# A mixture-of-experts stage: the overflow branch late, pair units first, the fixed experts' gather in halves

## The chip, the core and the metric

The kernel runs on one core of a Trainium2 chip. The metric is the device time of one execution in microseconds (us). The engines are TensorE (PE), VectorE (DVE), ScalarE (ACT), GpSimd (POOL) and SyncE (SP). Each takes its own instructions in the order of its queue and waits for the others through semaphores.

## What is computed

A backbone of two layers over 512 tokens of width 1024, all in float32. Each layer has a token mixer (attention and spatial gating in layer 0, a short convolution in layer 1) and then a mixture of experts. Only the mixture is touched by the change:

```python
g_idx = argmax(h @ w_rg + b_rg)                       # one of 4 groups
top_v, top_i = top_k(e_logits[group g_idx], 2)        # 2 of its 8 experts
gate = softmax(g_logits)[g_idx] * softmax(top_v)
for each expert e, over the tokens sent to it:
    hid = silu(x @ w_gate[e]) * (x @ w_up[e])         # 1024 -> 512
    y   = hid @ w_down[e]                             # 512 -> 1024
out[token] += gate * y
lat = lat + g2 * out
```

There are 32 experts per layer with 6 MB of weights each (w_gate and w_up as two tiles of 1 MB each, w_down as two), so 384 tiles of 1 MB for the two layers. 1024 assignments are spread over the 32 experts by the router, so how many tokens an expert has is known on the chip only.

## The kernel before

`channel` runs once per layer: `finish_mixer` ends the mixer's output projection, makes the normalised tokens `hv`, `lv` (high and low part), routes them (`Route.block`, `rank`) and starts the loads of the two fixed experts; `experts` then streams the experts' weights.

**Units.** The experts are sorted by their count on the chip. Line 30's PLAN is a row of letters, one per unit: F is one of two fixed experts (64 slots, weights loaded ahead), T one expert with 128 slots, S one with 64, C a pair of experts with 32 slots each. Units are worked off in the order of the letters. `gather` (L1132 ff., products on L1147) brings the tokens of a group of units together with a one-hot product: 64 matmul instructions for 256 slots, then `inform` for weights and token numbers. `up` (L1220, for a T unit L1226) is the first product, of 4 tiles per expert in two halves of two; `mid` transposes and applies SiLU (L1235 to L1245, for T to L1257); `down` (L1274) is the second product, of 2 tiles per expert, and its result is scattered into `acc` in DRAM by an indirect DMA on POOL (L966). In the loop of `experts` unit i does `up(i)`, `down(i-1)`, a few steps of the next gather, `mid(i)`.

**The ring.** `loaded` (L1188 to L1207) issues each weight tile on SP into a ring of 11 slots: two in a `big` buffer (a pair of tiles), five in `raw` buffers, four in two more `big` buffers. A slot is free when PE has read the tile that was in it; the buffers of one pool go round in the order of allocation. A stage has 180 such tiles, besides the 12 tiles of the two fixed experts that `finish_mixer` loads (L741): five into raw buffers, four into two big ones, three into wp buffers. A DMA also waits until the one eight places before it on SP has landed, since SP's DMAs take eight semaphores in turn.

**The overflow branch.** Where an expert has more tokens than its slots, `overflow` (L969 ff.) works off the rest in loops. Each engine loads the count `ovi` into a register (L973) and jumps over the loops if it is zero (L974). With these inputs it is zero in both layers. Before the change it stands ahead of unit 3, and its weight tile `w` is one of the raw buffers.

**The fixed experts' gather.** `gather_first` (L1095 ff.) makes the one-hot product for both fixed experts in two halves of 512 columns (L1105), copies them to `rows` (ACT L1110, DVE L1108), transposes eight blocks (L1120) and modulates them: the second four on ACT (L1090), the first four by two DVE passes over all of them (L1125, L1127). Between them stands the rest of the sort (`Route.sort`, L894 to L962): the slot tables X and info, and the overflow count.

Of the kernel before, what the change touches and what calls it, by code (L numbers as in the profile page):

```python
# [9 lines left out]
F32 = mybir.dt.float32  # L10
# [4 lines left out]
OP = mybir.AluOpType  # L15
# [10 lines left out]
FIX = 2  # L26
RING = 11


PLAN = "FF SCSC TSC SSC TSC SSC TC SCSS".replace(" ", "")  # L30
SLOTS, WIDTH, UNITS = [], [], []
_next = {"F": 0, "T": 2, "S": 5, "C": 16}
for _c in PLAN:
# [59 lines left out]
def backbone_kernel(ctx: ExitStack, tc: tile.TileContext, a, out):  # L93
# [723 lines left out]
    class Route:  # L817
# [77 lines left out]
        def sort(self, ep):  # L895
            tl, rt, xdg, cnt = self.tl, self.rt, self.xdg, self.cnt

            def bc(x, n):
                return x[:, :, None].to_broadcast([128, 4, n])

            kc = tl([128, 1], "kc")
            V.scalar_tensor_tensor(kc[0:96], cnt[0:96, 32:33], 32.0, C("kbcol")[0:96], op0=OP.mult, op1=OP.add)
            kr = tl([128, 32], "kr")
            V.scalar_tensor_tensor(kr[0:96], cnt[0:96, 0:32], 32.0, C("kbrow")[0:96], op0=OP.mult, op1=OP.add)
            V.tensor_scalar(kr[0:96], kr[0:96], kc[0:96], None, op0=OP.is_gt)
            pos = tl([128, 1], "pos")
            V.tensor_reduce(pos[0:96], kr[0:96], AX.X, OP.add)
            perm = tl([128, 3, 32], "perm", bufs=1)
            V.memset(perm, 0.0)
            for j in range(3):  # L910
                q = slice(32 * j, 32 * j + 32)
                V.tensor_scalar(perm[q, j, :], C("rank")[q], pos[q], None, op0=OP.is_equal)
            yield
            po = bankB()
            T.matmul(po[0:1, 0:32], lhsT=C("iop")[0:32], rhs=perm[0:32, 0, :], start=True, stop=True)
            T.matmul(po[0:1, 32:64], lhsT=cnt[0:32, 32:33], rhs=perm[0:32, 0, :], start=True, stop=True)
            V.tensor_copy(rt["ordi"], po[0:1, 0:32])
            ov = tl([1, 32], "ov")
            V.tensor_tensor(ov, po[0:1, 32:64], C("cap")[0:1], OP.subtract)
            yield  # L920
            V.tensor_copy(xdg[:, :, 32:64], bc(C("tok"), 32))
            e2 = tl([128, 4], "e2")
            A.activation(e2, self.dm, AF.Exp)
            gw = tl([128, 4], "gw")
            V.reciprocal(gw, self.gs)
            den = tl([128, 4], "den")
            V.tensor_scalar(den, e2, 1.0, None, op0=OP.add)
            V.reciprocal(den, den)
            w1 = tl([128, 4], "w1")
            V.tensor_tensor(w1, gw, den, OP.mult)  # L930
            w2 = tl([128, 4], "w2")
            V.tensor_tensor(w2, w1, e2, OP.mult)
            V.tensor_tensor(self.A1, self.A1, bc(w1, 32), OP.mult)
            V.tensor_tensor(self.A2, self.A2, bc(w2, 32), OP.mult)
            V.tensor_tensor(xdg[:, :, 64:96], self.A1, self.A2, OP.add)
            px = bankB()
            for b in range(NB):
                T.transpose(px[0:96, b * 128:(b + 1) * 128], xdg[:, b, :], ident)
            xT = ep.tile([128, 512], F32, tag="gy", name="xTr", bufs=2)
            A.activation(xT[0:96], px[0:96], AF.Copy)  # L940
            pq = bankB()
            pqv = pq[:, :384].rearrange("p (b c) -> p b c", b=4)
            for b in range(NB):
                T.matmul(pqv[:, b, :], lhsT=xT[0:96, b * 128:(b + 1) * 128],
                         rhs=perm[0:96].rearrange("p a b -> p (a b)"), start=True, stop=True)
            V.tensor_copy(rt["X"], pqv[:, :, 0:32])

            def infos(dst, n, ix, wt):
                V.tensor_copy(dst[:, :, :, 0], ix)
                A.activation(dst[:, :, :, 1], wt, AF.Copy)  # L950
                V.tensor_tensor(dst[:, :, :, 2], wt, dst[:, :, :, 1].bitcast(F32), OP.subtract)
                V.tensor_copy(dst[:, :, :, 3], one[:, :, None].to_broadcast([128, 4, n]))

            infos(rt["info"], 32, pqv[:, :, 32:64], pqv[:, :, 64:96])
            infos(rt["infoF"], FIX, xdg[:, :, 32:32 + FIX], xdg[:, :, 64:64 + FIX])
            ovc = ep.tile([1, 32, 8], F32, tag="gy", name="ovc", bufs=2)
            V.tensor_tensor(ovc, ov[:, :, None].to_broadcast([1, 32, 8]), C("c64")[0:1, None, :].to_broadcast([1, 32, 8]),
                            OP.is_gt)
            nx = tl([1, 33], "nx")
            V.tensor_reduce(nx[:, 0:32], ovc, AX.X, OP.add)  # L960
            V.tensor_reduce(nx[:, 32:33], nx[:, 0:32], AX.X, OP.add)
            V.tensor_copy(rt["ovi"], nx)  # L962

    def scatter(acc, y, ix):

# [3 lines left out]
    def overflow(l, ep, hv, lv, rt, acc):  # L969

        X, info, ordi, ovi = rt["X"], rt["info"], rt["ordi"], rt["ovi"]
        why = "a count or an index made on the chip"
        any_over = nc.values_load(ovi[0:1, 32:33], min_val=0, max_val=256, skip_runtime_bounds_check_because=why)  # L973
        with pool("o%d" % l, 1) as op, tc.If(any_over > 0):  # L974
# [6 lines left out]
            ixi = op.tile([64, 1], I32)  # L981
            xw = wp.tile([128, 2048], F32, name="wp")
            xt = xw[:, 0:512].rearrange("p (k s) -> p k s", k=8)
            w = rawp.tile([128, 2048], F32, name="raw")
            sl = ep.tile([64, 512], F32, tag="gy", name="slo", bufs=2)
            ht = ep.tile([128, 4, 64], F32, tag="ht", name="hto")
            y = ep.tile([64, 1024], F32, tag="gy", name="yo", bufs=2)
# [52 lines left out]
    def experts(l, ep, ec, hv, lv, early, rt, acc, following):  # L1040
# [46 lines left out]
            def modulated(o, src, k, on_act):  # L1087
                g, h = gcol[:, k:k + 1], scol[:, k:k + 1]
                if on_act:
                    A.activation(o, src, AF.Identity, scale=g, bias=h)  # L1090
                else:
                    V.tensor_scalar(o, src, g, h, op0=OP.mult, op1=OP.add)  # L1092

            def gather_first():

# [2 lines left out]
                onehot(O, 0, 0, FIX, 64)  # L1098
                rows = ep.tile([64 * FIX, 1024], F32, tag="gy", name="rows", bufs=2)
                pa = bankA()  # L1100
                for half in range(2):
                    c = slice(half * 512, half * 512 + 512)
                    for b in range(NB):
                        for h, src in enumerate((hv, lv)):
                            T.matmul(pa[0:n, c], lhsT=O[:, b, :], rhs=src[:, b, c], start=(b == 0 and h == 0),  # L1105
                                     stop=(b == 3 and h == 1))
                    if half:
                        V.tensor_copy(rows[:, c], pa[0:n, c])  # L1108
                    else:
                        A.activation(rows[:, c], pa[0:n, c], AF.Copy)  # L1110
                    take(rt["sorting"], 1)
                xt = wp.tile([128, 2048], F32, name="wp")
                x = xt[:, 0:8 * n].rearrange("p (k s) -> p k s", k=8)
                for q in range(8 * n // 512):
                    pt = bankB()
                    m = 512 // n
                    ks = slice(m * q, m * q + m)
                    for j in range(m):
                        k = m * q + j
                        T.transpose(pt[:, j * n:j * n + n], rows[:, k * 128:(k + 1) * 128], ident[0:n, 0:n])  # L1120
                    if q % 2:
                        for j in range(m):
                            modulated(x[:, m * q + j], pt[:, j * n:j * n + n], m * q + j, True)
                        continue
                    V.tensor_tensor(x[:, ks], pt.rearrange("p (k s) -> p k s", k=m),  # L1125
                                    gcol[:, ks, None].to_broadcast([128, m, n]), OP.mult)
                    rt["x"] = V.tensor_tensor(x[:, ks], x[:, ks], scol[:, ks, None].to_broadcast([128, m, n]), OP.add)  # L1127
                for e in range(FIX):
                    state[e] = [[x[:, :, 64 * e:64 * e + 64]], None, None]
                return O  # L1130
# [184 lines left out]
            rt["sorting"] = rt["sort"](ep)  # L1315
            take(rt["sorting"], 1)
            O = gather_first()
            take(rt["sorting"], 9)

            g2h = ec.tile([128, 512], F32, name="g2h")  # L1320

            g2q = ec.tile([128, 512], F32, name="g2q")
            with tc.issue_after(rt["x"].ins):
                for h in range(2):
                    q = slice(64 * h, 64 * h + 64)
                    V.tensor_copy(g2h[q], g2b[q, 512 * h:512 * h + 512])
# [2 lines left out]
                    V.tensor_copy(g2q[q], g2b[q, 512 * (h % 2):512 * (h % 2) + 512])  # L1329
            prev = None  # L1330
            for i, u in enumerate(UNITS):
                if i == FIX + 1:
                    overflow(l, ep, hv, lv, rt, acc)
                tiles = [source(j) for j in u]
                if i == 0:
                    source(FIX)
                    pg = up(u, tiles)
                    with tc.issue_after(rt["x"].ins):
# [18 lines left out]
                pg = up(u, tiles)  # L1357
                down(*prev)
                if i < FIX:
                    with tc.issue_after(rt["x"].ins):  # L1360
                        take(ahead, 9 if i == FIX - 1 else 0)
                else:
                    steps(i, 3)
# [192 lines left out]
```

## Time and profile before

| what | us |
|---|---|
| median of 3 runs | 1606.33 (1606.21 to 1606.42) |
| the profiled execution | 1607.4 |
| its span | 1605.7 |
| PE busy | 1422.3 (89%) |
| DVE busy | 535.7 (33%) |
| ACT busy | 354.7 (22%) |
| POOL busy | 101.5 (6%) |
| DMA | 508.28 MB, mean 317 GB/s |

All times in the trace are counted from the start of the span. Busy time on PE is modelled and pipelined, so a high share there does not say by itself that PE is the limit. The expert stages lie at about 320 to 832 us (layer 0) and 1069 to 1579 us (layer 1). In the views of stretches a row gives the stretch, its width, the busy time of PE, PE's weight loads, DVE, ACT and POOL with the count of instructions, the granted clock as a share of 2.4 GHz, the mean share of the 16 DMA engines and the GB/s. In SP's timeline a row is an issue (or a run of them), not a transfer; the time until landing is a view of its own. In the chain a row with DMA runs from a transfer's issue to its landing.

### The profile page before, as it was taken

The page shows a single profiled execution, that of the slowest core. Times are in us where ns is not written, and L with a number is a line of the kernel's source. Part 1 is how long each engine was busy: PE and PEld are TensorE (multiplying, and loading weights), DVE is VectorE, ACT ScalarE, POOL GpSimd, SP SyncE. Part 2 cuts the span into 40 slices and gives each one's busy share as a digit, 9 for nine tenths or more (in the row PEclk, how much of TensorE's full clock was granted, in tenths as well). Part 3 has the DMA queues.
Part 4 walks back from the last instruction along what each step waited for, and adds up shares of the span by engine and source line. Part 5 has one row for each costly group of instructions (what it writes and reads, how often), then busy time and mean ns, then how long its engine had stood idle before and what let it go on. Part 6 is the DMA issues. An engine that isn't in the chain of part 4 may idle for free. (4 is left out here: it accounts for less than half of the span.)

```text
span 1605.7 us, 18697 instructions
## 1 busy us (share of the span) xinstructions
PE 1422.3 (89%) x7260; PEld 771.7 (48%) x7261; DVE 535.7 (33%) x1099; ACT 354.7 (22%) x630; POOL 101.5 (6%) x84
## 2 busy tenths in 40 slices
PE   6899989899899898987778999989889989898875
PEld 2777668755343233432127888855434424233212
DVE  6778885631111100100018874461111101000003
ACT  6657463311010000000015333321101000000001
POOL 0000000000010101101100000000011011011000
PEclk9899999898999999999898999989999999899898
DMA  9235565647999999999994763264999999999994
GB/s 364 110 143 195 186 247 197 236 162 318 409 413 405 412 414 405 410 416 411 408 392 166 271 233 129 85 264 182 375 410 408 412 413 414 408 413 414 413 417 185
DMA packets 78672, 508.28 MB, mean 317 GB/s; under 512 B 11535, under 2 KB 11919, under 8 KB 19824
## 3 DMA queue, kind: packets, MB, share of 16 engines
q1 hardware_dynamic: 71984, 499.09, 77.0%
q0 software_dynamic: 6592, 7.92, 2.8%
q8 instruction: 59, 0.97, 0.2%
q14 instruction: 37, 0.30, 0.0%
HBM read 492.77 MB, written 19.40 MB: 319 GB/s over the span
## 5 line engine op out<-in xcount | busy, mean ns | idle before, releaser
L1220 PE MATMUL pa<-big,wp 128*32 128x512 f32 (+1 forms) x944 | 270.0, 662 | 39.5 <-DMA big<-in_wexp_dram 39.3
L1220 PE MATMUL pa<-raw,wp 128*64 128x512 f32 (+1 forms) x896 | 255.0, 659 | 40.9 <-DMA raw<-in_wexp_dram 35.9
L1147 PEld LDWEIGHTS pb<-O,big 128*128 128x128 f32 x896 | 115.7, 197 | 73.0 <-issue 69.6
L966 POOL DMA_INDIRECT acc<-y,ixi x60 | 89.7, 1495 | 942.3 <-DVE y L1281 779.0
L1147 PE MATMUL pb<-O,big 128*128 128x256 f32 (+2 forms) x896 | 132.3, 295 | 13.4 <-DVE O L1048 13.4
L1220 PEld LDWEIGHTS pa<-big,wp 128*32 128x32 f32 (+1 forms) x944 | 64.0, 130 | 165.0 <-issue 90.4
L1281 DVE SCALAR_TENSOR_TENSOR y<-pa,g,g2h 128x512 f32<-128x512 f32 x26 | 19.5, 751 | 366.7 <-PE pa L1274 366.7
L1220 PEld LDWEIGHTS pa<-raw,wp 128*64 128x64 f32 (+1 forms) x896 | 61.5, 132 | 160.7 <-issue 84.9
L1235 ACT ACTIVATE gs<-pa 128x512 f32<-128x512 f32 x42 | 25.1, 597 | 452.2 <-PE pa L1220 452.2
L1274 PE MATMUL pa<-big,ht 128*32 128x512 f32 (+1 forms) x528 | 108.8, 623 | 12.1 <-DMA big<-in_wexp_dram 12.0
L140 DVE TENSOR_TENSOR wp<-raw,wp 128x1024 fp32r<-128x1024 f32 x70 | 84.0, 1221 | 36.1 <-ACT wp L139 35.6
L205 DVE SCALAR_TENSOR_TENSOR acc<-raw,csil,acc 128x1024 f32<-128x1024 f32 x70 | 89.4, 1279 | 0.5
L1274 PE MATMUL pa<-raw,ht 128*32 128x512 f32 (+1 forms) x368 | 80.6, 627 | 9.7 <-DMA raw<-in_wexp_dram 5.8
L139 ACT ACTIVATE wp<-raw 128x1024 fp32r<-128x1024 f32 x70 | 72.0, 1053 | 43.3 <-PE pb L259 17.0
L1092 DVE TENSOR_SCALAR wp<-pb,gcol,ada 128x256 f32<-128x256 f32 (+2 forms) x56 | 28.7, 515 | 148.3 <-PE pb L1147 128.1
L1090 ACT ACTIVATE wp<-pb,ada,gcol 128x256 f32<-128x256 f32 (+2 forms) x64 | 33.1, 530 | 187.6 <-PE pb L1147 166.7
L257 PE MATMUL pb<-big,wp 128*128 128x512 f32 x168 | 65.6, 391 | 0.0
L259 PE MATMUL pb<-big,wp 128*128 128x512 f32 x168 | 65.4, 389 | 0.0
L258 PE MATMUL pb<-big,wp 128*128 128x512 f32 x168 | 65.4, 389 | 0.0
L1274 PEld LDWEIGHTS pa<-big,ht 128*32 128x32 f32 (+1 forms) x528 | 26.1, 121 | 76.9 <-issue 51.7
L1242 ACT ACTIVATE sl<-pb 128x256 f32<-128x256 f32 x42 | 16.1, 382 | 189.9 <-PE pb L1238 180.0
L1281 DVE SCALAR_TENSOR_TENSOR y<-pa,g,g2q 128x512 f32<-128x512 f32 x16 | 12.0, 751 | 130.1 <-PE pa L1274 130.1
(319 smaller groups left out, 1983.9 us busy)
## 6 DMA issues: line engine op xcount, KB each, us to landing
big<-in_wexp_dram SPq DMA_DIRECT2D x204, 1024.0 KB, 20.0
raw<-in_wexp_dram SPq DMA_DIRECT2D x174, 1024.0 KB, 20.0
raw<-in_wada_dram SPq DMA_DIRECT2D x48, 1024.0 KB, 5.2
raw<-in_win_dram SPq DMA_DIRECT2D x19, 1024.0 KB, 6.4
raw<-in_wout_dram SPq DMA_DIRECT2D x8, 1024.0 KB, 5.7
wp<-in_wexp_dram SPq DMA_DIRECT2D x6, 1024.0 KB, 8.2
big<-in_x_dram SPq DMA_DIRECT2D x8, 512.0 KB, 8.0
acc<-big SPq DMA_DIRECT2D x8, 512.0 KB, 2.6
```

The costliest lines, as they stand in the source:

```text
L139: A.activation(h, src, AF.Copy)
L140: V.tensor_tensor(l, src, h.bitcast(F32), OP.subtract)
L205: V.scalar_tensor_tensor(acc, src, csil[:, k, 0:1], acc, op0=OP.mult, op1=OP.add)
L257: T.matmul(po, lhsT=sH, rhs=mH, start=first, stop=False)
L258: T.matmul(po, lhsT=sH, rhs=mL, start=False, stop=False)
L259: T.matmul(po, lhsT=sL, rhs=mH, start=False, stop=last)
L966: G.indirect_dma_start(out=acc, out_offset=bass.IndirectOffsetOnAxis(ap=ix, axis=0), in_=y, in_offset=None, bounds_check=acc.shape[0] - 1, ...
L1090: A.activation(o, src, AF.Identity, scale=g, bias=h)
L1147: T.matmul(pg[:, :n], lhsT=src[:, b, k * 128:(k + 1) * 128], rhs=O[:, b, 0:n], start=(h == 0 and b == 0), stop=(h == 1 and b == 3))
L1220: T.matmul(pg[w * q:w * q + w, 0:512], lhsT=x[q // 2][:, k, :], rhs=ws[q][:, kk * 512:kk * 512 + 512], start=(k == 0), stop=(k == 7))
L1274: T.matmul(po, lhsT=ht[:, k, e, :], rhs=ws[e][:, c:c + 512], start=(k == 0), stop=(k == 3))
L1281: V.scalar_tensor_tensor(y, py[:, 0:512], gt, g2q if w == 32 else g2h, op0=OP.mult, op1=OP.mult)
```

## The change

Four things are edited.

- **PLAN**: the same letters (2 F, 3 T, 11 S, 8 C) in another order. After the fixed units come two pairs; the last four units are as before.
- **The overflow branch** moves from ahead of unit 3 to ahead of unit 21 of 0 to 23. Just ahead of it the loop issues the ten tiles that `up(21)` and `down(20)` need. The overflow count is made inside `overflow` and no longer in the sort, and the branch's weight tile comes from the wp pool.
- **`gather_first`**: each half of `rows` is transposed and modulated by itself, blocks in turn on DVE and ACT; the unit's first product can then begin on the first half.
- **The sort** makes the fixed experts' info first and, behind a new `yield`, the tables X and info for the others; these are issued after the last modulated blocks.

```diff
@@ PLAN
-PLAN = "FF SCSC TSC SSC TSC SSC TC SCSS".replace(" ", "")
+PLAN = "FF CCSC TSSC TSC SST CSSC SCSS".replace(" ", "")
@@ Route.sort
+            rt["ov"] = ov
...
+            infos(rt["infoF"], FIX, xdg[:, :, 32:32 + FIX], xdg[:, :, 64:64 + FIX])
             px = bankB()
...
+            yield
             V.tensor_copy(rt["X"], pqv[:, :, 0:32])
...
-            infos(rt["infoF"], FIX, xdg[:, :, 32:32 + FIX], xdg[:, :, 64:64 + FIX])
-            ovc = ep.tile([1, 32, 8], F32, tag="gy", name="ovc", bufs=2)
...
-            V.tensor_copy(rt["ovi"], nx)
@@ overflow
+        ovc = ep.tile([1, 32, 8], F32, tag="gy", name="ovc", bufs=2)
...
+        V.tensor_copy(ovi, nx)
         why = "a count or an index made on the chip"
         any_over = nc.values_load(ovi[0:1, 32:33], min_val=0, max_val=256, skip_runtime_bounds_check_because=why)
...
-            w = rawp.tile([128, 2048], F32, name="raw")
+            w = wp.tile([128, 2048], F32, name="wp")
@@ gather_first
+                def chunks(half):
+                    pt = bankB()
+                    for j in range(4):
+                        k = 4 * half + j
+                        T.transpose(pt[:, j * n:j * n + n], rows[:, k * 128:(k + 1) * 128], ident[0:n, 0:n])
+                    for j in range(4):
+                        rt["x", j % 2] = modulated(x[:, 4 * half + j], pt[:, j * n:j * n + n], 4 * half + j, j % 2).ins
...
+                    if half:
+                        chunks(0)
+                chunks(1)
-                xt = wp.tile([128, 2048], F32, name="wp")
...
-                    V.tensor_tensor(x[:, ks], pt.rearrange("p (k s) -> p k s", k=m),
-                                    gcol[:, ks, None].to_broadcast([128, m, n]), OP.mult)
-                    rt["x"] = V.tensor_tensor(x[:, ks], x[:, ks], scol[:, ks, None].to_broadcast([128, m, n]), OP.add)
@@ experts
-            take(rt["sorting"], 9)
+            with tc.issue_after(rt["x", 0]), tc.issue_after(rt["x", 1]):
+                take(rt["sorting"], 9)
...
-                if i == FIX + 1:
-                    overflow(l, ep, hv, lv, rt, acc)
-                tiles = [source(j) for j in u]
+                tiles = [source(j) for j in u]
+                if i == len(UNITS) - 3:
+                    for t in range(2):
+                        for tl in tiles:
+                            for o in (t, 2 + t):
+                                tl[o] = (loaded(tl[o]),)
+                    for t in (4, 5):
+                        for tl in prev[1]:
+                            tl[t] = (loaded(tl[t]),)
+                    overflow(l, ep, hv, lv, rt, acc)
```

Three places show the order. The first is on DVE, from the copy of the second half of `rows` on, in layer 0 (`wp` is the fixed experts' gathered input, `X` and `info` the slot tables, `g2h` a copy for a later step). Before:

```order
L1108 COPY rows<-pa 128x512
L946 COPY X<-pb 128x128
L949 CAST info<-pb 128x128
L957 TENSOR_TENSOR ovc<-ov,cst 1x256
L951 TENSOR_TENSOR info<-pb,info 128x128
L960 TENSOR_REDUCE nx<-ovc 1x32
L961 TENSOR_REDUCE nx<-nx 1x1
L962 CAST ovi<-nx 1x33
L1125 TENSOR_TENSOR wp<-pb,gcol 128x512
L1127 TENSOR_TENSOR wp<-wp,ada 128x512
L1326 COPY g2h<-g2b 64x512 x2
```

With the change:

```order
L1120 COPY rows<-pa 128x512
L1093 TENSOR_SCALAR wp<-pb,gcol,ada 128x128 x4
L956 COPY X<-pb 128x128
L939 CAST info<-pb 128x128
L942 CAST info<-cst 128x128
L1326 COPY g2h<-g2b 64x512
L941 TENSOR_TENSOR info<-pb,info 128x128
L1326 COPY g2h<-g2b 64x512
L1329 COPY g2q<-g2b 32x512 x4
```

The four blocks now stand directly behind the copy, the sort's tables behind them, and the overflow count is gone from here.

The second is the head of the stage, on PE from unit 0's second product on (`big,ht`). Before:

```order
L1274 MATMUL pa<-big,ht 64x512 x8
L1147 MATMUL pb<-O,big 128x256 x64
L1163 MATMUL pb<-info,O 64x4 x16
L1220 MATMUL pa<-big,wp 64x512
L1069 MATMUL pb<-r,cst 128x8
L1238 MATMUL pb<-cst,gs 128x128 x4
L1220 MATMUL pa<-big,wp 64x512 x7
```

With the change:

```order
L1273 MATMUL pa<-big,ht 64x512 x8
L1146 MATMUL pb<-O,big 128x256 x64
L1162 MATMUL pb<-info,O 64x8 x16
L1219 MATMUL pa<-big,wp 32x512 x2
L1219 MATMUL pa<-raw,wp 32x512 x2
L1219 MATMUL pa<-big,wp 32x512
L1071 MATMUL pb<-r,cst 128x8
L1237 MATMUL pb<-cst,gs 128x128 x3
```

The gather behind unit 0 is now that of pairs, and unit 2's first product, of 32 slots, reads four tiles at a time in place of two. On SP, from the ring's third tile on (`raw_3128` and `raw_3122`), before:

```order
L1206 ISA
L1206 DMA raw_3128<-in_wexp_dram 128x2048
L1206 ISA
L1206 DMA raw_3130<-in_wexp_dram 128x2048
L973 TENSOR_LOAD ovi_2205
L974 COMPARE_AND_BRANCH
...
L1017 ISA
L1017 DMA raw_3301<-in_wexp_dram 128x2048
```

With the change:

```order
L1205 ISA
L1205 DMA raw_3122<-in_wexp_dram 128x2048
L1205 ISA
L1205 DMA raw_3124<-in_wexp_dram 128x2048
L1205 ISA
L1205 DMA raw_3142<-in_wexp_dram 128x2048
L1205 ISA
L1205 DMA raw_3144<-in_wexp_dram 128x2048
L1205 ISA
L1205 DMA raw_3146<-in_wexp_dram 128x2048
L1205 ISA
L1205 DMA big_3148<-in_wexp_dram 128x2048
```

The register load of the branch and its raw buffer (`raw_3301`) no longer stand between the raw tiles.

The third is the late branch on SP with its waits (DMAHW0 to 7 are the eight semaphores of SP's DMAs), with the change only; before, nothing but tiles stands there:

```order
L1205 DMA big<-in_wexp_dram 128x2048 [waits DMAHW0_49,PE_49]
L1205 ISA
L1205 DMA big<-in_wexp_dram 128x2048 [waits DMAHW1_49]
L1205 ISA
L1205 DMA big<-in_wexp_dram 128x2048 [waits DMAHW2_49,PE_49]
L975 TENSOR_LOAD ovi [waits DVE_49]
L976 COMPARE_AND_BRANCH
L990 COMPARE_AND_BRANCH
L990 UNCONDITIONAL_BRANCH [waits SP_sequencer_49,DMAHW0_49,DMAHW3_49,DMAHW4_49,DMAHW5_49,DMAHW6_49,DMAHW7_49]
...
L1183 TENSOR_LOAD ordi
L1205 ISA
L1205 DMA big<-in_wexp_dram 128x2048 [waits DMAHW3_49]
```

The last three of the ten tiles issued ahead stand above the branch; the path that skips it waits for six of the eight semaphores, all but the two of the last two tiles.

## Rows read from the trace of the kernel before

**Rows 1.** Page, section 2: DMA busy tenths in 40 slices of the span
```profile
DMA  9235565647999999999994763264999999999994
```

**Rows 2.** Stretches, layer 1: width, PE, PEld, DVE, ACT, POOL busy, PEclk, DMA share, GB/s
```profile
1077.00:1083.00 6.00, 6.00 (x18) 1.62 (x16) 2.90 (x10) 0.00 (x0) 0.00 (x0) 0.60 0.00 0
1083.00:1096.00 13.00, 13.00 (x62) 4.52 (x60) 0.81 (x3) 2.86 (x4) 0.00 (x0) 1.00 0.85 323
1096.00:1115.00 19.00, 19.00 (x128) 12.18 (x126) 5.30 (x15) 2.64 (x5) 1.60 (x1) 1.00 0.02 2
...
1130.00:1142.00 12.00, 8.85 (x69) 5.71 (x72) 2.83 (x6) 0.95 (x2) 0.00 (x0) 0.73 0.81 330
...
1164.00:1579.00 415.00, 362.14 (x1689) 136.30 (x1681) 43.18 (x99) 29.95 (x57) 40.00 (x27) 0.95 1.00 406
```

**Rows 3.** Stretches, layer 0, same columns
```profile
329.00:333.00 4.00, 4.00 (x16) 1.21 (x14) 1.93 (x8) 0.00 (x0) 0.00 (x0) 0.76 0.00 0
...
346.00:365.00 19.00, 19.00 (x128) 12.29 (x126) 5.29 (x15) 2.64 (x5) 1.73 (x1) 1.00 0.08 10
...
414.00:832.00 418.00, 363.71 (x1694) 134.81 (x1694) 43.15 (x99) 29.95 (x57) 40.17 (x27) 0.95 1.01 409
```

**Rows 4.** SP's timeline, layer 1: start, us to the group's end, line, names, count
```profile
1083.04 3.20 SPq L1206 DMA_DIRECT2D raw<-in_wexp_dram  x2
1090.51 0.33 SPq L1206 DMA_DIRECT2D raw<-in_wexp_dram  x1
1114.95 0.34 SPq L1206 DMA_DIRECT2D raw<-in_wexp_dram  x1
...
1130.19 0.33 SPq L1206 DMA_DIRECT2D raw<-in_wexp_dram  x1
```

**Rows 5.** SP's waits: who waited for whom, us in total, times, longest
```profile
SPq L1206 <- PE pa L1220: 269.6, 65, 23.6
...
SPq L1206 <- PEq L974: 20.3, 2, 10.4
```

**Rows 6.** Line 1206: issue to landing of its DMAs
```profile
DMA to landing us min/median/max: 4.8/20.2/23.2
```

**Rows 7.** PE's timeline at the stage's head: start, us, line, shapes, count, idle before
```profile
326.77 8.78 PE L1220 MATMUL pa<-raw,wp 128*64 128x512 f32 x32 [2.35 <-DVE wp L1127]
...
1075.76 10.07 PE L1220 MATMUL pa<-raw,wp 128*64 128x512 f32 x32 [2.35 <-DVE wp L1127]
...
1098.11 7.83 PE L1147 MATMUL pb<-O,big 128*128 128x256 f32 x64
...
1106.75 1.07 PE L1220 MATMUL pa<-big,wp 128*64 128x512 f32 x2
```

**Rows 8.** Chain that ended last, in order of time: start, us, what
```profile
1137.71 7.10 PE pa L1220 x64
...
1146.41 17.37 DMA big<-in_wexp_dram
...
1189.84 3.58 PE pa L1274 x16
...
1194.25 13.73 PE pa L1226 x32
...
1220.66 7.02 PE pa L1220 x32
1227.68 7.06 PE pa L1274 x16
...
1549.34 19.97 DMA big<-in_wexp_dram
```

**Rows 9.** DMA issues from 1146.40 to 1549.30: names, count, KB, median us to landing
```profile
big<-in_wexp_dram SPq DMA_DIRECT2D x84, 1024.0 KB, 20.7
raw<-in_wexp_dram SPq DMA_DIRECT2D x70, 1024.0 KB, 20.4
```

**Rows 10.** Line 974, PE's sequencer: ns min/median/max, first and last start
```profile
L974 PEldq COMPARE_BRANCH  x2: 368/390/412, 379.5 to 1129.6; - x2
```

More of the change, by code (lines that the diff above doesn't have):

```diff
@@ L935, in sort, with infos @@
             V.tensor_tensor(xdg[:, :, 64:96], self.A1, self.A2, OP.add)
+            def infos(dst, n, ix, wt):
+                V.tensor_copy(dst[:, :, :, 0], ix)
+                A.activation(dst[:, :, :, 1], wt, AF.Copy)
+                V.tensor_tensor(dst[:, :, :, 2], wt, dst[:, :, :, 1].bitcast(F32), OP.subtract)
+                V.tensor_copy(dst[:, :, :, 3], one[:, :, None].to_broadcast([128, 4, n]))
+            infos(rt["infoF"], FIX, xdg[:, :, 32:32 + FIX], xdg[:, :, 64:64 + FIX])
             px = bankB()
@@ L945, in sort @@
                          rhs=perm[0:96].rearrange("p a b -> p (a b)"), start=True, stop=True)
+            yield
             V.tensor_copy(rt["X"], pqv[:, :, 0:32])
[L948 to L952, printed above, removed]
-            infos(rt["info"], 32, pqv[:, :, 32:64], pqv[:, :, 64:96])
-            infos(rt["infoF"], FIX, xdg[:, :, 32:32 + FIX], xdg[:, :, 64:64 + FIX])
-            ovc = ep.tile([1, 32, 8], F32, tag="gy", name="ovc", bufs=2)
[L957 to L961, printed above, removed]
-            V.tensor_copy(rt["ovi"], nx)
+            infos(rt["info"], 32, pqv[:, :, 32:64], pqv[:, :, 64:96])
     def scatter(acc, y, ix):
@@ L971, in overflow @@
         X, info, ordi, ovi = rt["X"], rt["info"], rt["ordi"], rt["ovi"]
+        ovc = ep.tile([1, 32, 8], F32, tag="gy", name="ovc", bufs=2)
+        V.tensor_tensor(ovc, rt["ov"][:, :, None].to_broadcast([1, 32, 8]), C("c64")[0:1, None, :].to_broadcast([1, 32, 8]),
+                        OP.is_gt)
+        nx = ep.tile([1, 33], F32, tag="nx", name="nx", bufs=1)
+        V.tensor_reduce(nx[:, 0:32], ovc, AX.X, OP.add)
+        V.tensor_reduce(nx[:, 32:33], nx[:, 0:32], AX.X, OP.add)
+        V.tensor_copy(ovi, nx)
         why = "a count or an index made on the chip"
@@ L1089, in modulated @@
                 if on_act:
-                    A.activation(o, src, AF.Identity, scale=g, bias=h)
-                else:
-                    V.tensor_scalar(o, src, g, h, op0=OP.mult, op1=OP.add)
+                    return A.activation(o, src, AF.Identity, scale=g, bias=h)
+                return V.tensor_scalar(o, src, g, h, op0=OP.mult, op1=OP.add)
             def gather_first():
@@ L1100, in gather_first @@
                 pa = bankA()
+                xt = wp.tile([128, 2048], F32, name="wp")
+                x = xt[:, 0:8 * n].rearrange("p (k s) -> p k s", k=8)
+                def chunks(half):
[5 more added lines that the diff above has]
+                        rt["x", j % 2] = modulated(x[:, 4 * half + j], pt[:, j * n:j * n + n], 4 * half + j, j % 2).ins
                 for half in range(2):
@@ L1111, in gather_first @@
                     take(rt["sorting"], 1)
-                xt = wp.tile([128, 2048], F32, name="wp")
[L1113 to L1124, printed above, removed]
-                    V.tensor_tensor(x[:, ks], pt.rearrange("p (k s) -> p k s", k=m),
-                                    gcol[:, ks, None].to_broadcast([128, m, n]), OP.mult)
-                    rt["x"] = V.tensor_tensor(x[:, ks], x[:, ks], scol[:, ks, None].to_broadcast([128, m, n]), OP.add)
+                    if half:
+                        chunks(0)
+                chunks(1)
                 for e in range(FIX):
@@ L1317, in experts @@
             O = gather_first()
-            take(rt["sorting"], 9)
+            with tc.issue_after(rt["x", 0]), tc.issue_after(rt["x", 1]):
+                take(rt["sorting"], 9)
             g2h = ec.tile([128, 512], F32, name="g2h")
             g2q = ec.tile([128, 512], F32, name="g2q")
-            with tc.issue_after(rt["x"].ins):
+            with tc.issue_after(rt["x", 0]):
                 for h in range(2):
@@ L1337, in experts @@
                     pg = up(u, tiles)
-                    with tc.issue_after(rt["x"].ins):
+                    with tc.issue_after(rt["x", 0]):
                         inform(UNITS[:FIX], O, [state[e][0][0] for e in range(FIX)])
@@ L1359, in experts @@
                 if i < FIX:
-                    with tc.issue_after(rt["x"].ins):
+                    with tc.issue_after(rt["x", 0]):
                         take(ahead, 9 if i == FIX - 1 else 0)
```

## The prediction

> **What bounds the kernel now.** I read the views in this order: the page's slices, the stretches around the start of each expert stage, SP's timeline there, SP's waits, and last the chain that ended last.
>
> The slices show the two expert stages as two long runs of full DMA share with a hole at the head of each [rows 1]. The stretches give the hole its size. In layer 1 the 415 us from 1164 to 1579 have a DMA share of 1.00 with PE busy 362 us: the weight stream sets the pace. Ahead of it the share is 0.00 for 6 us, 0.85 for 13, 0.02 for 19 and 0.81 for 12 [rows 2]. That is 6.0 + 1.9 + 18.6 + 2.3 = 28.8 us of DMA time lost. Layer 0 has the same shape: 4 us at 0.00, 19 us at 0.08, and then 418 us at 1.01 [rows 3]. So what ends a stage is the landing of its last tile, and a stage gets shorter by what the stream idles less ahead of it; what happens on PE inside the stream is free as long as slots of the ring come back in time.
>
> SP's timeline says why the stream idles. I count the ring's tiles from 0: tiles 0 and 1 go into the big buffer that the latent stream leaves, 2 to 6 into the five raw buffers that expert 0 and one tile of expert 1 leave, 7 to 10 into two big ones; tile 11 is the first that takes a tile's place of this ring. Tiles 3 and 4 are issued between 1083.04 and 1086.24, tile 5 at 1090.51, and tile 6 only at 1114.95, tile 14 at 1130.19 [rows 4]. By the code, the overflow branch allocates a raw buffer between tile 3 and tile 4; the raw buffers go round, so tile 6 does not get the fifth buffer that unit 1 leaves at about 1090 but waits for tile 2, which unit 2 reads until 1114.93, and tile 14 waits until PE has passed the branch. The waits agree: SP waited once in each layer, 20.3 us in all, for PE's branch, and up to 23.6 us for a product [rows 5].
>
> **The change part by part.** *The raw buffer and the order of the units.* With the branch at the end and its weights in a wp buffer, tiles 4, 5 and 6 get their own buffers, and tiles 7 to 10 follow as units 0 and 1 leave theirs, by some 1098 (the gather that follows unit 0's second product starts at 1098.11 [rows 7]) and not 1115 to 1118. The next limit is tile 11. It needs the first half of unit 2's first product, whose place on PE is after the same two fixed units and the same 64 gather products: 1106.75 before [rows 7]. Unit 2 is now a pair: its first product takes 7.10 us [rows 8], a half 3.55. Interleaved there are the transposes and small products of unit 1; before, that stretch lasted 1114.95 - 1106.75 = 8.2 us [rows 4, 7] against 7.02 of an S unit alone [rows 8], so 1.2. The half is done at 1106.75 + 3.55 + 1.2 = 1111.5. The fixed units start earlier by the next part, 2.3 us: 1109.2. A transfer that finds an empty queue lands 4.8 us after its issue [rows 6]: tile 11 lands at 1114.0. By then it stands in an unbroken stream: tiles 12 to 17 are freed by the same product, 18 to 21 by the first half of the next pair, some 16 us later, while seven tiles last 18 us.
>
> Before, tile 21 was issued at 1146.41 and landed 17.37 us later, at 1163.78; tile 175 landed at 1549.34 + 19.97 = 1569.31 [rows 8]; 84 + 70 = 154 issues lie between [rows 9], so a tile takes 405.53 / 154 = 2.63 us, scatters and all. On that line tile 11 belongs at 1163.78 - 10 x 2.63 = 1137.5. **The stream of layer 1 starts 1137.5 - 1114.0 = 23.5 us sooner**, of the 28.8 that idled. Layer 0 has the same sequence with less idle ahead (4 us for 6 [rows 2, 3]); I take 22.5. Sum 46.0.
>
> *The fixed experts' gather half by half.* Before, unit 0's first product waits 2.35 us with PE idle for the second of two DVE passes [rows 7], behind seven DVE instructions of the sort and the overflow count. After, DVE and ACT modulate each half as four blocks; the sort's instructions stand behind and the count's are gone from here. PE has no other work there, so 2.35 us is the most this wait can give, and the first half's two blocks per engine end before PE has done the products that stand ahead: 2.3 us taken, already in the sum above. The lower bound is 0.
>
> *The granted clock.* After that idle gap the clock was 0.60 from 1077 to 1083 and 1.00 from 1083 to 1096 [rows 2], 1.2 and 2.4 GHz. Unit 0's product took 10.07 us in layer 1 and 8.78 in layer 0 [rows 7], where 7.02 is an S unit's at full clock [rows 8]. If the gap goes, 3.1 + 1.8 = 4.9 us go with it, and all that follows up to tile 11 moves. Bounds 0 and 4.9; I take 4.9, since PE is busy at both sides of the gap.
>
> *The late branch.* It costs each engine a register load and a jump; PE's compare took 0.39 us [rows 10], in a unit for whose weights PE waits anyway. SP is the one to watch, and behind it stand all later loads. Ahead of the branch it now issues ten tiles: the pair's eight and two of the unit before. By the order's waits the path that skips the branch takes over six DMA semaphores, so SP stands there until all but two of those tiles have landed. Two tiles are 5.3 us of stream. Tiles 3 and 4 were issued within 3.20 us with the whole branch between them [rows 4], so SP's own part is under 2.9 us, and the next tile's bytes begin 4.8 - 2.6 = 2.2 us after its issue: 5.1 of 5.3 at the most. Taken 0.6 us a stage; bounds 0 and, with an empty queue, 5. POOL's scatters behind its branch are one per expert, 15.8 us apart, and lose nothing; the four small DVE steps that moved stand some units ahead, so nobody waits for the count.
>
> *The middle of the stage.* The three T units now lie within ten units (6 to 15: T S S C T S C S S T), before within thirteen. PE per unit with its share of a gather (7.83 for 64 products and, up to 1106.75, 0.8 for the slots' data [rows 7], a quarter of it, a half for T): T 13.73 + 7.06 + 1.3 + 4.3 = 26.4; S 7.02 + 3.58 + 0.6 + 2.2 = 13.4; a pair 13.5 [rows 8]. The ten: 79 + 67 + 27 = 173 us, against twelve experts of six tiles at 2.63, 189 us. Before: thirteen units, 79 + 80 + 54 = 213 against 268. The slack falls from 20% to 8%, and S S T alone is 53.2 on PE against 47.3. Seven or eight tiles under way cover that; taken 1.5 us a stage, bounds 0 and 4.
>
> *A thinner start.* Between tiles 11 and 18 the stream has 2 to 4 us in hand: taken 0.7 a stage, bounds 0 and 2. The end of the stage keeps its last three units, and the rest of the kernel is not touched.
>
> Sum: 46.0 + 4.9 - 2 x (0.6 + 1.5 + 0.7) = 45.3. The profiled execution took 1607.4 us (span 1605.7 and 1.7 around it): 1562.1. The median of the runs shown lies 1.1 under it: **1561 us**.
>
> **The rivals.** *PE runs out of slack in the middle.* Slots come back late in S S T, the stream breaks, and part of the head's gain is given back. For it: the 8% above, and 0.95 of granted clock over the stage, which makes 173 into 182. Against: before, where the same S S runs stand, the share stays at 1.00. With the upper bounds of this term and the thin start and no clock regained the gain is 46.0 - 2 x (4 + 2 + 0.6) = 33: 1573.
>
> *The same, so far that it is slower.* It decides once PE needs more than 189 + 23.5 = 213 us for the ten units, 1.23 times the full-clock sum, a granted clock of 0.81 throughout. At 1.3 times it is 225 us, 12 over per stage: 1606 + 2 x 12 = 1630. Against: a PE that bounds has no idle time, and where PE was busy throughout (1083 to 1115) the clock was 1.00 [rows 2].
>
> *The late branch breaks the stream.* Before, SP branched with an almost empty queue; now the queue is full. A jump itself was short: 0.39 us on PE [rows 10]. With SP late by a whole queue, the median of 20.2 us from issue to landing [rows 6] less the 5.3 that stay under way, a stage gives back 15 us: 1561 + 30 = 1591. The Trainium skill's page "Runtime: NRT & Kernel Launch", section "Instruction fetch mechanics", has a rule that would do this: a taken branch whose target lies outside the small window of code on the engine must fetch it by DMA before it goes on. The branch's body is as long as before, and the 0.39 us do not show such a fetch.
>
> *The buffer was not the limit.* If the head only fills up to tile 10 and tile 11 waits as long as tile 6 did (unit 2 slow, its gather late), little is gained: 10 us in all, 1596; at the extreme nothing, 1606.
>
> **How the numbers follow.** The forecast, 1554 to 1567: 0.62. PE's slack partly used, 1567 to 1580: 0.20. The late branch breaking the stream, 1580 to 1593: 0.07. Little or nothing gained: 0.07, of it 0.03 within 0.2%. Slower: 0.04. The range reaches from 1552 (no deduction: 1606.3 - 50.9 = 1555, and 3 for the terms taken from one layer) to 1578. About 0.2% is what a measurement of this kernel can tell from no change. Faster 0.93, same 0.03, slower 0.04.
>
> **What would show it.** Right: tile 6 issued some 4 us after tile 5; no stretch of DMA share near 0 longer than 6 us after tile 2; tile 21 landing some 23 to 26 us sooner against the stage's start; PE's first product without a wait for DVE, and no half clock in it; a DMA share of 1.00 from tile 11 to the end. Wrong: a dip of the share at the late branch, or in units 8 to 10 and 13 to 15 with SP waiting for L1220 there; a first product of 10 us as before; a stage that starts sooner and ends at the old distance.

## The result, and the profile after

The changed kernel takes **1562.4 us** (median of 4 runs, 1560.7 to 1562.7) against 1606.3 before: a ratio of 0.9725, 95% interval 0.9708 to 0.9742. The profiled execution took 1562.6 us, its span is 1560.9; 1607.4 and 1605.7 before. Taken from the issue of tile 0 to the landing of tile 179, the expert stage went from 512.2 to 488.9 us in layer 0 and from 509.8 to 489.1 in layer 1. Those 44.0 us are nearly all of the 44.8 by which the profiled executions differ.

The page's slices of DMA share after, to be held against [rows 1]: the hole at the head of both stages (slices 9 and 28, counted from 1) has filled.

```profile
DMA  9336465598999999999994763278999999999995
```

The stretches after (width, PE, PEld, DVE, ACT, POOL busy, PEclk, DMA share, GB/s) answer to [rows 2, 3]. Where 6 us at 0.00 and 19 us at 0.02 or 0.08 stood, one hole of 6 us is left in each layer, between tiles 10 and 11. Behind it the share is 1.00 to the end of the stage, as before.

```profile
1046.00:1056.00 10.00, 10.00 (x61) 5.21 (x60) 7.41 (x22) 2.20 (x5) 0.00 (x0) 1.00 0.78 278
1056.00:1061.00 5.00, 5.00 (x24) 1.97 (x24) 0.81 (x3) 2.26 (x3) 0.00 (x0) 1.00 1.02 429
1061.00:1079.00 18.00, 18.00 (x124) 11.31 (x120) 4.50 (x13) 2.86 (x5) 1.60 (x1) 1.00 0.92 374
1079.00:1085.00 6.00, 6.00 (x53) 2.39 (x56) 1.26 (x5) 0.38 (x1) 0.00 (x0) 1.00 0.11 19
...
1088.00:1535.00 447.00, 395.71 (x1942) 158.71 (x1938) 52.66 (x121) 36.01 (x68) 42.90 (x29) 0.95 1.00 403
...
353.00:359.00 6.00, 6.00 (x50) 2.21 (x49) 2.07 (x9) 0.38 (x1) 0.00 (x0) 1.00 0.09 18
363.00:809.00 446.00, 390.66 (x1942) 157.80 (x1940) 52.63 (x121) 36.01 (x68) 42.88 (x29) 0.96 1.01 407
```

SP's timeline in layer 1 (tiles 4 and 5, tile 6, tile 11): tile 6 goes out 4.1 us after tile 5, where it took 24.4 [rows 4]. Tile 11 now is the late one.

```profile
1056.36 0.92 SPq L1205 DMA_DIRECT2D raw<-in_wexp_dram  x2
...
1061.00 0.33 SPq L1205 DMA_DIRECT2D raw<-in_wexp_dram  x1
...
1083.16 0.33 SPq L1205 DMA_DIRECT2D big<-in_wexp_dram  x1
```

PE's timeline, unit 0's first product in layer 0 and in layer 1: 7.09 us in both, with no wait ahead of it; before 8.78 and 10.07, each behind 2.35 us of waiting for DVE [rows 7].

```profile
324.05 7.09 PE L1219 MATMUL pa<-raw,wp 128*64 128x512 f32 x32
...
1049.24 7.09 PE L1219 MATMUL pa<-raw,wp 128*64 128x512 f32 x32
```

SP's waits (in total, times, longest), to be held against [rows 5]: the longest wait for a first product fell from 23.6 to 13.1 us, the wait for PE's branch is gone, and SP stands at its own branch instead, once in each layer for nearly 15 us.

```profile
SPq L1205 <- PE pa L1219: 261.1, 71, 13.1
...
SPq L976 <- SPq L976: 30.6, 4, 14.9
```

### The profile page after: what moved, and what is told of

Read it like the earlier page. It is cut to its first block, busy times and chain, and to the rows that moved or that the text cites. A ratio compares the mean times of both kernels' runs of the same rounds, so it can differ in the third digit from the quotient of the medians.

```text
span 1560.9 us, 18692 instructions
## 1 busy us (share of the span) xinstructions
PE 1391.3 (89%) x7260; PEld 766.0 (49%) x7261; DVE 537.0 (34%) x1103; ACT 356.0 (23%) x630; POOL 100.9 (6%) x84
## 5 line engine op out<-in xcount | busy, mean ns | idle before, releaser
L1219 PE MATMUL pa<-big,wp 128*32 128x512 f32 (+1 forms) x992 | 274.8, 635 | 39.8 <-DMA big<-in_wexp_dram 33.2
L1219 PE MATMUL pa<-raw,wp 128*32 128x512 f32 (+1 forms) x848 | 237.7, 645 | 28.7 <-DMA raw<-in_wexp_dram 28.7
L1219 PEld LDWEIGHTS pa<-big,wp 128*32 128x32 f32 (+1 forms) x992 | 69.4, 127 | 158.3 <-issue 90.5
L1146 PEld LDWEIGHTS pb<-O,big 128*128 128x128 f32 x896 | 110.8, 189 | 60.0 <-issue 55.0
L1146 PE MATMUL pb<-O,big 128*128 128x256 f32 (+2 forms) x896 | 127.7, 288 | 0.0
L1219 PEld LDWEIGHTS pa<-raw,wp 128*32 128x32 f32 (+1 forms) x848 | 58.5, 128 | 128.4 <-issue 74.3
L1273 PE MATMUL pa<-raw,ht 128*32 128x512 f32 (+1 forms) x400 | 91.0, 661 | 17.6 <-DMA raw<-in_wexp_dram 13.5
L1093 DVE TENSOR_SCALAR wp<-pb,gcol,ada 128x256 f32<-128x256 f32 (+2 forms) x64 | 31.9, 501 | 193.1 <-PE pb L1146 170.9
```

What stands on the lines that cost most here:

```text
L1093: return V.tensor_scalar(o, src, g, h, op0=OP.mult, op1=OP.add)
L1146: T.matmul(pg[:, :n], lhsT=src[:, b, k * 128:(k + 1) * 128], rhs=O[:, b, 0:n], start=(h == 0 and b == 0), stop=(h == 1 and b == 3))
L1219: T.matmul(pg[w * q:w * q + w, 0:512], lhsT=x[q // 2][:, k, :], rhs=ws[q][:, kk * 512:kk * 512 + 512], start=(k == 0), stop=(k == 7))
L1273: T.matmul(po, lhsT=ht[:, k, e, :], rhs=ws[e][:, c:c + 512], start=(k == 0), stop=(k == 3))
```

## The experiments

Three parts went in together: where the branch stands and whose buffer it takes, the order of the units, and the gather in halves. The first seven runs take them apart; three look at what limits the head next. Each run is compared by its ratio to the kernel before, measured beside it.

### The buffer alone

```diff
 # kernel before
-w = rawp.tile([128, 2048], F32, name="raw")
+w = wp.tile([128, 2048], F32, name="wp")
```

> The kernel before with one line changed: the overflow branch takes its weights' buffer from wp, not from raw; branch, order and gather stay. If the raw buffer alone held the stream back, tile 6 is issued some 4 to 5 us after tile 5, tile 11 lands some 20 us sooner than on before's line in each stage, and the time is near 1606 - 2 x 20 = 1566. My theory, sharpened by the traces: the buffer only lets the stream run up to tile 14; unit 2 is one expert here and frees tiles 11 to 14 at its product (1111 to 1115 in before's trace), but tile 15 needs the first half of the pair of unit 3, which PE starts only at 1137.6 after two gathers and the branch. Tile 15 then lands near 1146, on before's line it belongs at 1137.5 + 4 x 2.63 = 1148: 0 to 4 us a stage gained, 1598 to 1606.

1606.8 us, ratio 1.0009 (1.0000 to 1.0019): nothing gained, where my theory had 0 to 4 us a stage. And yet the trace has what the prediction asked of this edit: tile 6 goes out 4.0 us after tile 5, tile 11 lands at 1114.6. The stretches of layer 1 show that the hole only moved behind tile 14:

```profile
1109.00:1124.00 15.00, 15.00 (x96) 9.72 (x93) 2.89 (x5) 2.29 (x4) 1.56 (x1) 1.00 0.73 284
1124.00:1140.00 16.00, 12.06 (x100) 8.08 (x102) 3.91 (x13) 1.51 (x3) 0.00 (x0) 0.79 0.01 4
1140.00:1146.00 6.00, 6.00 (x43) 1.77 (x32) 0.20 (x1) 0.60 (x1) 0.00 (x0) 1.00 0.98 406
```

PE's timeline says what tile 15 waits for. After the gather that unit 3 needs (64 products) PE reaches the branch; it then idles 3.15 us until DVE has made a one-hot, its own pass through the branch within them, and makes 24 products of the next gather, and only then starts the product of unit 3 that gives tile 15 its place.

```profile
1116.57 7.83 PE L1147 MATMUL pb<-O,big 128*128 128x256 f32 x64
...
1126.07 0.36 PE L1069 MATMUL pb<-r,cst 64*128 64x8 f32 x2 [0.79 <-DVE r L1065]
...
1130.66 4.50 PE L1147 MATMUL pb<-O,big 128*128 128x256 f32 x24 [3.15 <-DVE O L1048]
1135.10 0.63 PE L1220 MATMUL pa<-raw,wp 128*32 128x512 f32 x3
```

### The branch late, with either buffer

```diff
 # kernel before; and a second time without the wp line
-if i == FIX + 1:
+if i == len(UNITS) - 3:
     overflow(l, ep, hv, lv, rt, acc)
...
-w = rawp.tile([128, 2048], F32, name="raw")
+w = wp.tile([128, 2048], F32, name="wp")
```

> The kernel before with the branch ahead of the last three units and its weights in wp; order of units and gather as before. The early branch with its weights in wp gave 1606.8, this with the new gather 1579.6, and the new gather is worth 7.1 by its own run. If the branch's place is what gained the rest: 1579.6 + 7.1 = 1587. In the trace the tile that waited for PE's branch in before (tile 14) and tile 15 behind it come some 10 us sooner. If the place does nothing and the new gather and the place only act together: 1600 to 1606.

1588.0 us, ratio 0.9888 (0.9871 to 0.9904), as the first theory had it. PE's timeline, the same place: the gather ends, and unit 3's product follows at once; the 24 products of the next gather come after it.

```profile
1106.48 7.83 PE L1147 MATMUL pb<-O,big 128*128 128x256 f32 x64
...
1115.12 0.63 PE L1220 MATMUL pa<-raw,wp 128*32 128x512 f32 x3
...
1127.94 3.10 PE L1147 MATMUL pb<-O,big 128*128 128x256 f32 x24
```

From the end of the 64 products to unit 3's product it is 0.8 us here, 10.7 with the early branch. Tile 15 is issued 62.8 us after tile 0, against 71.8: 9.0 us a stage, and 18 us in all is what the clock says.

> The same as the run beside it, but with the branch's weights in a raw buffer as in before. The raw buffers go round, so from the branch on one raw tile in each lap waits for a tile only four raw tiles back, with some 18 tiles of the stage to come. My reading of before, that such a slip breaks the stream where it stands, asks for a break after the branch of some 5 to 10 us a stage: 1597 to 1607. If the slip costs nothing where the stream is full: 1585 to 1589.

1586.9 us, ratio 0.9877 (0.9861 to 0.9893): the buffer's kind costs nothing late either, and my expectation of a break was wrong. SP does wait for PE's branch, but with a full queue nobody notices:

```profile
SPq L1206 <- PEq L974: 12.6, 2, 7.5
```

### The order of the units undone

```diff
 # changed kernel
-PLAN = "FF CCSC TSSC TSC SST CSSC SCSS"
+PLAN = "FF SCSC TSC SSC TSC SSC TC SCSS"
```

> The changed kernel with the order of units of before (FF SCSC TSC SSC TSC SSC TC SCSS); late branch, wp buffer and the gather in halves stay. My theory: without a pair at the start tile 15 waits for the first half of unit 3, which stands behind two gathers; without the branch (3.15 us of waiting there) and with the 5 us that the gather in halves and the clock give, it lands some 10 to 12 us sooner than in before and 11 to 13 later than in after: 1580 to 1588. If the buffer is what counts and the order does nothing, 1561 to 1566, and less than that if the three T units closer together cost time in after.

1579.6 us, ratio 0.9843 (0.9828 to 0.9858), just under my theory's range. The order is worth 0.9843 - 0.9725 = 0.0118, 19 us. In layer 1 tile 15 is issued 57.9 us after tile 0, against 40.4 in the changed kernel: with one expert in unit 2, a second gather of 64 products stands on PE ahead of unit 3's product, which gives tile 15 its place. With a pair in unit 2, unit 2's own product does that.

```profile
1076.95 7.86 PE L1146 MATMUL pb<-O,big 128*128 128x256 f32 x64
...
1097.96 7.77 PE L1146 MATMUL pb<-O,big 128*128 128x256 f32 x64
...
1106.55 0.63 PE L1219 MATMUL pa<-raw,wp 128*32 128x512 f32 x3
```

The early branch with the pairs first was not tried on the chip, so what the order gives without the late branch is not known.

### The gather whole

The changed kernel with the old `gather_first` and without the `issue_after` ahead of the sort's last steps. The sort's new order stays, and the overflow count stays out of it.

```diff
-    if half:
-        chunks(0)
-chunks(1)
+for q in range(8 * n // 512):
+    ...
+    if q % 2:
+        ...  # ACT, block by block
+        continue
+    V.tensor_tensor(x[:, ks], ..., OP.mult)
+    rt["x", 0] = V.tensor_tensor(x[:, ks], ..., OP.add).ins
```

> The changed kernel with the gather of the fixed experts as before (all rows first, then the transposes, DVE in two passes over half the chunks, ACT the other half); order of units, late branch and wp buffer stay. My theory: PE waits about 2.3 us for DVE again ahead of the first product, the clock falls for some 3.4 to 6.8 us (1.8 us lost in layer 0, 3.1 in layer 1), and every tile up to 11 comes later by that: 1562.4 + 4.6 + 4.9 = 1572, at least 1567 if the clock does not fall. The rival, that the halves buy nothing because the stream is held by something else at its head: 1561 to 1564.

1569.5 us, ratio 0.9771 (0.9756 to 0.9786): 0.0046 or 7 us above the changed kernel, 7.1 by the medians, between the two values of my theory. PE waits for DVE again and works through part of the product at the lower clock. The row of layer 1 (layer 0 has the same wait and the same 8.78 us), and the stretch at its start:

```profile
1057.19 8.78 PE L1221 MATMUL pa<-raw,wp 128*64 128x512 f32 x32 [1.63 <-DVE wp L1128]
```
```profile
1057.00:1060.00 3.00, 2.81 (x8) 0.95 (x10) 2.87 (x9) 0.00 (x0) 0.00 (x0) 0.55 0.50 202
```

1.63 of waiting and 8.78 - 7.09 = 1.69 of clock are 3.3 us; two stages, 6.6. The three parts add up: late branch 0.0112, halves 0.0046, order 0.0118, together 0.0276 of the 0.0275 measured. The sum checks one thing only, that the halves are worth the same with the old order (0.9888 - 0.9843 = 0.0045) as with the new one; the late branch was taken with the old order, and the order with the late branch.

### The ten tiles ahead of the branch, and the branch itself

```diff
 # changed kernel, first run
-for t in range(2): ... tl[o] = (loaded(tl[o]),)
-for t in (4, 5): ... tl[t] = (loaded(tl[t]),)
 # second run: these and
-overflow(l, ep, hv, lv, rt, acc)
```

> The changed kernel without the ten tiles that are issued ahead of the late branch. My theory: SP's register load at the branch waits for DVE's count, which stands in DVE's order behind the product of the unit before; that ends when all that was issued has landed and been used. So the queue runs empty: some 10 to 14 us a stage for the rest of that product, its activation and the 4.8 us of a lone tile, 1582 to 1590. If the ten tiles are no cover that is needed (the count is early and SP goes past the branch as it did in before): 1560 to 1565.

> The changed kernel without the overflow branch, its count and the tiles ahead of it (it leaves out the work on tokens beyond an expert's slots, of which this input has none, so only the asking for it is gone). By the landings in after's trace the stream does not break at the branch: 1560 to 1563. If SP's 14.9 us of standing there cost what I had put on it or more (0.6 to 5 us a stage): 1552 to 1561; the sum's own value would be 1561.2.

Without the ten tiles 1562.7 us, ratio 0.9728 (0.9713 to 0.9743): the same. My theory fell. SP reads its register and branches early, at 1447.0 and not 1473.0, some tiles earlier in its order; it stands as long in all, in 14 short waits and not in 4.

```profile
L976 SPq COMPARE_BRANCH  x2: 45/48/50, 720.2 to 1447.0; - x2
```
```profile
SPq L976 <- SPq L976: 30.8, 14, 3.3
```

Without the branch 1560.0 us, ratio 0.9710 (0.9697 to 0.9723): the two intervals overlap, so whether the late branch costs anything is not settled. The medians differ by 2.4 us, and all five executions without it (1557.4 to 1560.6) are shorter than the four of the changed kernel (1560.7 to 1562.7). The same 22 us around the branch, the changed kernel and the one without:

```profile
1468.00:1490.00 22.00, 14.10 (x62) 2.91 (x58) 2.46 (x4) 0.38 (x1) 2.84 (x2) 0.81 0.87 354
```
```profile
1468.00:1490.00 22.00, 14.85 (x62) 2.93 (x58) 1.17 (x2) 0.38 (x1) 2.84 (x2) 0.80 1.02 416
```

The share does dip, while SP stands and only two tiles are left under way. But the last tile ahead of the gap in SP's issues and the first behind it, 17.1 us apart at their issue, land 2.5 us apart: SP is back just in time.

### What limits the head next

The first edit lets PE make chunks 0 to 3 of unit 2's gather, then the first half of its product, then the rest. The second and third also hold back the gather of the single experts, behind the first half of unit 3's product and behind all of it.

```diff
 # changed kernel
-take(ahead, 9 if i == FIX - 1 else 0)
+take(ahead, 4 if i == FIX - 1 else 0)   # up() takes the rest between its halves
...
 # second run: rt["up", 0], third run: rt["up", 1], the last product of a half
-steps(i, 3)
+with tc.issue_after(rt["up", 1]):       # for unit 3; none of it after unit 2
+    steps(i, 3)
```

> The changed kernel with one more edit: the gather that follows unit 0's second product makes its chunks 0 to 3, then PE does the first half of unit 2's first product (it reads only these), then chunks 4 to 7 and the second half. If PE's order of work is what leaves the stream idle for 5.6 and 6.5 us between tiles 10 and 11, tile 11 is issued some 3.9 us sooner (half of 7.83 us); tile 18, which waits for the first half of unit 3's product, keeps its place on PE, and the 1.8 us that the stream idles there become up to 5: a gain of 1 to 4 us a stage, 1554 to 1560. If tile 18 alone sets the pace of the head, the same 1562 within 1; if it pushes PE's work back, 1563 to 1566.

1562.4 us, ratio 0.9730 (0.9716 to 0.9743): the same, as the rival with tile 18 had it. Tile 11 is issued 6.4 us sooner against tile 0, and the hole at tile 11 is gone; it stands at tile 18 now, 7 us at 0.42:

```profile
1080.00:1096.00 16.00, 16.00 (x122) 9.01 (x120) 4.96 (x17) 2.67 (x5) 1.56 (x1) 1.00 0.98 400
1096.00:1103.00 7.00, 7.00 (x52) 3.74 (x50) 0.83 (x2) 0.56 (x1) 0.00 (x0) 1.00 0.42 141
```

> The version with unit 2's gather in halves and one more edit: PE makes the next gather (64 products, for the single experts) only behind the first half of unit 3's product, where before 43 of the 64 stood ahead of that half's end. With the halves alone tile 11 came 7.1 and 6.4 us sooner and the time stayed, so PE's way to unit 3's product is the next limit. If that is so, tiles 18 to 21 are issued 5 to 7 us sooner, tile 22 (it waits for the second half, behind the whole gather now) 4 to 6 us: 3 to 4 us a stage, 1554 to 1557. If PE only pushes its work into the stream's slack and something else sets the stage's end: 1561 to 1564.

> The same as the run beside it, but PE makes that gather behind all of unit 3's product. Then tiles 18 to 21 are issued some 7 us sooner against the stage's start than in after, 22 to 25 some 10 us sooner (they wait for the landing of tile 15, not for the gather), and the stream runs without a break from tile 11 or 12 on: 4 to 6 us a stage, 1550 to 1555. The rival: unit 4's product comes later by the gather that now stands ahead of it, and the tiles that wait for it break the stream there: 1556 to 1564.

1554.0 us, ratio 0.9678 (0.9665 to 0.9692), and **1549.1 us, ratio 0.9641** (0.9623 to 0.9658): both are faster than the changed kernel, the first by 8 us, the second by 13 (its executions spread from 1544.3 to 1552.6), and it is the best version here. The first lies at the edge of its range, the second just under its own. Its stretches in layer 1, from tile 1 on, have no hole of the old size left:

```profile
1046.00:1074.00 28.00, 28.00 (x162) 12.28 (x161) 9.25 (x27) 6.38 (x12) 1.60 (x1) 1.00 0.90 363
1074.00:1099.00 25.00, 25.00 (x198) 12.37 (x200) 5.21 (x16) 2.68 (x5) 1.56 (x1) 1.00 0.99 391
1099.00:1113.00 14.00, 12.90 (x94) 8.60 (x87) 4.30 (x11) 2.57 (x5) 1.42 (x1) 0.93 1.02 422
```

So PE's order of work at the head is what bounds the changed kernel. The first edit alone gave nothing; the gain came as the products of unit 3, which free the next places, moved ahead of a gather that nobody waited for yet.

## Why the prediction was right, and where it was not

**The time and the state at the end: right.** 1562.1 was the sum for the profiled execution, 1562.6 came. The reading that the stage ends with the stream and that the idle head is what can be gained fits the runs. Tile 21 lands 23.6 and 24.4 us sooner against tile 0, inside the 23 to 26 named. Tile 11 was to land 41.4 us after the issue of tile 0 (44.5, less 3.1 of clock); it landed at 43.1 and 42.6. That the sum came within 0.5 us has some luck in it: by its terms layer 0 should have gained 22.5 + 1.8 - 2.8 = 21.5 us and layer 1 23.5 + 3.1 - 2.8 = 23.8, and the stages gained 23.3 and 20.7; the two misses nearly cancel.

**The cause of the 23.5 us: wrong in part.** The sum put them on the raw buffer and the order, and charged the late branch 0.6 us. The buffer alone gave nothing, early or late. That the branch leaves the head gave 18 us, two fifths of the whole. The step that failed is the reading of the waits: SP's two waits for PE's branch [rows 5] were taken as a delay of tile 14 alone. What the branch did to PE was not asked: it parted PE's work in two, so that 24 products of a later gather and a wait for DVE stood ahead of unit 3, 10.7 us from the gather to unit 3's product where the late branch leaves 0.8. Before's trace had that, in a row of PE's timeline that the prediction passed over:

```profile
1133.20 4.51 PE L1147 MATMUL pb<-O,big 128*128 128x256 f32 x24 [3.15 <-DVE O L1048]
```

The total came out because the prediction worked out the state after all the edits, tile by tile from PE's order (tiles 18 to 21 "some 16 us later": 16.6), and there the branch no longer stands; that sum needs no split among the edits. Had only the buffer been changed, the same argument would have promised 20 us a stage for an edit that gave none.

**The gather in halves: right in kind, a third too large for the halves alone.** The wait and the low clock are gone as said. The prediction had 2.3 + 3.1 and 2.3 + 1.8 us, 9.5 in all, and against before the rows lose that much: 2.35 us of waiting in each layer, 1.69 and 2.98 of the product, 9.4. But undone by itself it costs 7. The wait that comes back is 1.63 us and not 2.35: from the copy of `rows` to the end of its second pass DVE takes 3.6 us there, 4.3 before, as the overflow count no longer stands between. And layer 1 loses 1.69 us to the clock and not 2.98; why it lost more before is open.

**The late branch:** 0.6 us a stage taken; the medians put it at 1.2, within the noise. SP stood until all but two tiles had landed, as worked out from the order. That the ten tiles ahead are needed as its cover was not borne out. The jump was as short as before: PE's compare took 338 ns and SP's 50, as the changed kernel's line 976 shows. A compare's own time need not be the whole jump, so the next instruction counts too: SP's starts 0.50 and 0.45 us after its compare starts, and 0.50 and 0.44 before the change.

```profile
L976 PEldq COMPARE_BRANCH  x2: 323/338/352, 741.4 to 1467.7; - x2
...
L976 SPq COMPARE_BRANCH  x2: 50/50/50, 746.5 to 1473.0; - x2
```

The Trainium skill's page "Runtime: NRT & Kernel Launch", section "Instruction fetch mechanics", says that a taken branch whose target lies outside the window of code on the engine must fetch it first. This trace shows no such wait; whether the target lies outside that window here, it does not tell.

**The middle and the thin start.** The rival that PE runs out of slack did not come: the share is 1.00 or 1.01 from tile 11 on. The stream did break at tile 18 by 1.8 us in layer 0 and not in layer 1, where 0.7 was taken for each. From tile 21's landing to the last one, layer 0 takes 418.5 us as before (418.3), layer 1 419.3 and not 415.5. Those 3.8 us are spread over the whole stage with the share at 1.02: the tiles move more slowly in some stretches. With the old order of units and all the rest of the change they don't, so most of it goes with the order. Without the branch layer 1 takes 417.7, so up to 1.6 of the 3.8 may be the branch's. Why the order slows the tiles is open. The same 80 us of the stage, the changed kernel and the one with the old order:

```profile
1200.00:1280.00 80.00, 77.52 (x388) 35.27 (x387) 12.15 (x31) 7.38 (x14) 7.48 (x5) 0.96 1.02 407
```
```profile
1220.00:1300.00 80.00, 69.91 (x341) 26.00 (x334) 8.45 (x20) 5.96 (x12) 7.51 (x5) 0.96 1.02 411
```

**What would show it.** One of the signs of a wrong forecast, a dip of the share at the late branch, is there (0.87) and cost little, if anything; it was the wrong thing to look at, since a tile counts when it lands.

## What to carry to other kernels

When a stream waits for buffers, list for each late tile the product that frees it and look at what else stands ahead of that product on its engine; here one buffer more for the stream only moved the hole to the next tile whose product was late. Ask also what a branch keeps apart on each engine: here what stood behind it on PE cost 9 us a stage, the branch itself little. Work out the state after all edits rather than a price for each, and if you must say which edit pays, run each alone.

## What the runs showed of the hardware

The clock of PE fell to its lower level, 1.2 GHz, behind a wait of only 1.10 us in layer 1 (0.50 granted from 1109 to 1112), while the same wait in layer 0 left it whole (1.00 from 384 to 387). That the wait is the cause is not shown; small products stood around it in both layers. The two waits, and the stretches behind them:

```profile
382.31 0.36 PE L1071 MATMUL pb<-r,cst 64*128 64x8 f32 x2 [1.10 <-DVE r L1067]
...
1107.50 0.36 PE L1071 MATMUL pb<-r,cst 64*128 64x8 f32 x2 [1.10 <-DVE r L1067]
```
```profile
384.00:387.00 3.00, 3.00 (x36) 0.91 (x32) 0.00 (x0) 0.60 (x1) 0.00 (x0) 1.00 1.01 423
...
1109.00:1112.00 3.00, 3.00 (x19) 0.69 (x15) 0.00 (x0) 0.00 (x0) 0.00 (x0) 0.50 1.02 421
```

And in layer 1, with SP standing until two 1 MB tiles were left under way, the DMA engines' mean share fell to 0.87 over 22 us, and yet the next four tiles (164 to 167) landed within 0.1 us of where they landed in the run without the branch, at 1495.9 to 1503.4.
